# A four-layer hybrid decoder trunk on one core: small tiles moved to a pool of their own, and the activations' tiles shifted to another offset in SBUF

## The chip, the cores and the metric

The kernel runs on one core of one Trainium2 chip. The metric is the device time of one execution in microseconds. A profiled execution has a span, from its first to its last instruction, and a time of its own that is a little longer.

## The reference, cut to what matters

Four residual layers over 256 tokens of width 1024. Layer `i` has a token mixer (latent attention, a Conformer convolution module, HGRN2, attention again), then a SwiGLU feed-forward block and a gated per-layer embedding. Nearly all of the arithmetic is dense products of the 256 tokens with weights in float32:

```python
for i in range(DEPTH):
    u = _rmsnorm(h, norm1_g[i])
    h = h + mixer(u)                      # MLA, Conformer, HGRN2, MLA
    h = h + _swiglu(_rmsnorm(h, norm2_g[i]), ffn_w_gu[i], ffn_w_down[i])
    gate = jax.nn.sigmoid(_rmsnorm(h, ple_norm_g[i]) @ ple_w_gate[i])
    h = h + (p[i] @ ple_w_proj[i]) * gate
return _rmsnorm(h, final_norm_g)

def _swiglu(u, w_gu, w_down):
    gate, up = jnp.split(u @ w_gu, 2, axis=-1)
    return (jax.nn.silu(gate) * up) @ w_down
```

The widths are 1024 for the model, 2816 for the feed-forward block, 256 for the embedding.

## The kernel before, in words

The 256 tokens are two tiles of 128 rows (`NT`). The residual stream stays in SBUF as `h0` and `h1`. Every float32 product is made from three reduced-precision products: an operand is split into a high part and a low part of type `float32r`, and `mm` (L221) issues high x high, high x low and low x high into the same PSUM bank.

Weights are streamed. `granule` (L177) loads up to 1024 columns of a weight matrix into `raw` by SyncE's DMA queue; ScalarE writes the high part `whi` (L189, or L194 with the norm's gain), VectorE the low part `wlo` (L190, L195). There are 4 slots of `raw`, 9 of `whi` and 8 of `wlo`, each of 4096 bytes in a partition, in the pool `wpool`.

Activations are transposed on TensorE (`split_T`, L250) and split the same way into pairs of tiles: `xT` (the normalised stream, and the mixers' outputs), `aT` (the feed-forward block's hidden part), `cT` (attention's low-rank part) and `pT` (the embedding input). In most products a 128x128 block of an activation's tile is the stationary operand, which a weight load (LDWEIGHTS) brings into the array, and 512 columns of `whi` or `wlo` are the moving operand. In the Conformer's first product and in HGRN2's q and f projections it is the other way round: a block of the weights is stationary and 256 columns of `xT` move. Each matmul has a weight load of its own. The feed-forward block alternates, for each of 11 pieces, 24 matmuls for each token tile into the bank `mm` (from `xT`) with 12 into the banks `acc` (from `aT`).

Where the tiles lie: a pool's slots lie one behind the other in the order in which their tags are first asked for, each rounded up to 32 bytes of a partition, and the pools lie in the order in which they are opened: `const`, `wpool`, `act`, and then, at the same place again and again, the scope of the current stage. In the kernel before that gives these offsets in a partition, modulo 256 bytes:

- `whi`, `wlo`, `raw`: 224 (and all their slots, since a slot has 4096 bytes)
- `h0`, `h1`, `junk`: 224
- `xT`, `pT`, `pph`: 96
- `th`, `hg`, `gain`: 160
- the stage's scope begins at 160, and with it `aT` and `cT`

The odd offsets come from seven tags of very small tiles (one to four numbers in a partition: `ss`, `sst`, `rs_m`, `rs_y`, `rs_h`, `rs_t`, `rhalf`), which `tmp` (L158) claims from `act` among the large ones. Their 960 bytes lie partly ahead of `xT`, partly between it and `pph`, partly behind. All blocks that a matmul takes from these tiles begin at a multiple of 256 bytes from the tile's begin, so the offset of the tile is that of each block.

Of the kernel before, what the change touches and what calls it, by code (L numbers as in the profile page):

```python
# [12 lines left out]
F32 = mybir.dt.float32  # L13
# [8 lines left out]
P = 128  # L22
# [29 lines left out]
GAINS = {}  # L52
for _k in GSIZE:
    GAINS[_k] = sum(GSIZE[j] * GCOUNT[j] for j in GAINS)


class Norm:
# [3 lines left out]
    def __init__(self, T, full=False, defer=False):  # L61
        self.T, self.full, self.defer = T, full, defer
        self.x, self.r = None, [None] * NT
# [64 lines left out]
class Trunk:  # L128
    def __init__(self, ctx, tc, a, out):
        self.ctx, self.tc, self.nc, self.a, self.out = ctx, tc, tc.nc, a, out  # L130
        nc = self.nc
        pool = lambda name, **k: ctx.enter_context(tc.tile_pool(name=name, **k))
        self.const = pool("const", bufs=1)
        self.wpool = pool("wpool", bufs=1)
        self.act = pool("act", bufs=1)
        self.ps = pool("ps", bufs=1, space=PSUM)
        self.n = 0
        self.fence = []
        self.head = None
        self.pinned = False  # L140
        self.pT, self.pph = {}, {}
        self.ident = self.const.tile([P, P], F32, name="ident")
        make_identity(nc, self.ident)
        self.gT = self.const.tile([P, a["gains"].shape[1]], F32, name="gT")
        self.h = [self.act.tile([P, D], F32, name=f"h{t}", tag=f"h{t}") for t in range(NT)]

    def nm(self, s):
# [8 lines left out]
        return self.bank("acc", 4)  # L156

    def tmp(self, tag, shape, bufs, dtype=F32, pool=None):  # L158
        return (pool or self.act).tile(shape, dtype, name=self.nm(tag), tag=tag, bufs=bufs)

    def scope(self, name):
        return self.tc.tile_pool(name=name, bufs=1)
# [404 lines left out]
    def mla(self, i, norm, done, pre):  # L567
# [8 lines left out]
        with self.scope(self.nm("mla")) as pool:  # L576
# [5 lines left out]
            for t in range(NT):  # L582
                xs, r = self.cut(norm.x, t), norm.r[t]
                pa, pb = self.acc(), self.acc()
                self.mms(pa[:, :QL], xs, [(hi[:, 0, :QL], lo[:, 0, :QL]) for hi, lo in gr])
                self.mms(pb[:, : KVL + ROPE], xs, [(hi[:, 0, QL : NC + ROPE], lo[:, 0, QL : NC + ROPE]) for hi, lo in gr])
                cg = tmp("cg", [P, NC], 1)
                nc.scalar.activation(cg[:, :QL], pa[:, :QL], AF.Copy)
                V.tensor_copy(cg[:, QL:], pb[:, :KVL])
                ss = tmp("css", [P, 2], 2)  # L590
                for c, (ps, n) in enumerate([(pa, QL), (pb, KVL)]):
                    nc.scalar.activation(self.tmp("junk", [P, 512], 1, BF16)[:, :n], ps[:, :n], AF.Square, scale=r, accum_out=ss[:, c : c + 1])
                kr = tmp("kr", [P, 1, ROPE], 2)
                nc.scalar.activation(kr[:, 0], pb[:, KVL : KVL + ROPE], AF.Copy, scale=r)
                self.split_T(cg, cT, 0, t)
                css.append(ss)
                krot.append(kr)
# [579 lines left out]
```

## Time and profile before

| | |
|---|---|
| median of 3 runs | 1401.75 us (1401.49 to 1403.82) |
| the profiled execution | 1402.8 us, of which 1401.0 us are its span |
| TensorE, matmuls | 1352.4 us busy, 97% of the span, 7153 of them |
| TensorE, weight loads | 1096.6 us, 78% |
| VectorE | 919.4 us, 66% |
| ScalarE | 789.7 us, 56% |
| DMA | 228.15 MB, 163 GB/s in the mean |

A matmul's duration in the profile reaches beyond the start of the next one, since matmuls are pipelined; what a matmul costs in a stream is the distance from its start to the next one's start. The profile's timeline merges neighbours of one kind into one row with a count.

### The profile page before, as it was taken

The page shows a single profiled execution, that of the slowest core. Times are in us where ns is not written, and L with a number is a line of the kernel's source. Part 1 is how long each engine was busy: PE and PEld are TensorE (multiplying, and loading weights), DVE is VectorE, ACT ScalarE, POOL GpSimd, SP SyncE. Part 2 cuts the span into 40 slices and gives each one's busy share as a digit, 9 for nine tenths or more (in the row PEclk, how much of TensorE's full clock was granted, in tenths as well). Part 3 has the DMA queues.
Part 4 walks back from the last instruction along what each step waited for, and adds up shares of the span by engine and source line. Part 5 has one row for each costly group of instructions (what it writes and reads, how often), then busy time and mean ns, then how long its engine had stood idle before and what let it go on. Part 6 is the DMA issues. An engine that isn't in the chain of part 4 may idle for free.

```text
span 1401.0 us, 20409 instructions
## 1 busy us (share of the span) xinstructions
PE 1352.4 (97%) x7153; PEld 1096.6 (78%) x7153; DVE 919.4 (66%) x1995; ACT 789.7 (56%) x1494; POOL 19.1 (1%) x52
## 2 busy tenths in 40 slices
PE   7899999999898999999999999999999999999997
PEld 6767878887875788887788887878878767888885
DVE  6867555558876855556887768555567776655556
ACT  6776555546525654555675546555556776555543
POOL 0100000000000000000000000000000000000000
PEclk9999999999998999999999999999999999999999
DMA  7524656536564655554474425555553433665532
GB/s 234 176 67 128 201 175 191 188 123 220 182 181 153 196 181 180 181 180 163 122 211 132 133 91 175 185 181 181 180 169 110 139 121 108 217 189 187 188 119 74
DMA packets 174023, 228.15 MB, mean 163 GB/s; under 512 B 11712, under 2 KB 138848, under 8 KB 173920
## 3 DMA queue, kind: packets, MB, share of 16 engines
q1 hardware_dynamic: 173920, 226.85, 51.6%
q8 instruction: 56, 0.92, 0.3%
q14 instruction: 47, 0.39, 0.1%
HBM read 222.27 MB, written 1.05 MB: 159 GB/s over the span
## 4 chain that ended last, share of the span: by engine, by line
PE 77%; DVE 8%; DMA 6%; ACT 6%; issue 2%; SPq 0%; DVEq 0%; ACTq 0%
PE mm L216 42%; PE acc L216 26%; PE tr L259 3%; DVE wlo L195 3%; ACT whi L194 2%; DMA raw<-in_ple_w_gate_dram 1%; PE acc L1020 1%; DMA raw<-in_conv_w_pw_dram 1%; DMA raw<-in_mla_w_in_dram 1%; DMA raw<-in_ffn_w_down_dram 1%; PE acc L659 1%; ACT p L669 1%; PE tr L641 1%; DVE wlo L190 1%; ACT whi L189 1%
## 5 line engine op out<-in xcount | busy, mean ns | idle before, releaser
L216 PE MATMUL mm<-whi,xT 128*128 128x512 f32 x1632 | 553.4, 402 | 1.0 <-ACT xT L246 0.7
L194 ACT ACTIVATE whi<-raw,gT 128x512 fp32r<-128x512 f32 (+3 forms) x604 | 387.7, 700 | 136.4 <-PE acc L216 60.1
L195 DVE SCALAR_TENSOR_TENSOR wlo<-raw,gT,whi 128x512 fp32r<-128x512 f32 (+3 forms) x604 | 410.4, 729 | 60.3 <-PE acc L216 33.9
L216 PEld LDWEIGHTS mm<-whi,xT 128*128 128x128 f32 x1632 | 306.3, 189 | 67.1 <-ACT xT L246 1.2
L216 PE MATMUL mm<-wlo,xT 128*128 128x512 f32 x816 | 323.7, 397 | 1.1 <-DVE wlo L190 1.1
L216 PE MATMUL acc<-whi,aT 128*128 128x512 f32 x704 | 234.5, 394 | 1.6 <-DVE aT L247 1.6
L190 DVE TENSOR_TENSOR wlo<-raw,whi 128x1024 fp32r<-128x1024 f32 x120 | 146.4, 1223 | 73.1 <-ACT whi L189 72.7
L189 ACT ACTIVATE whi<-raw 128x1024 fp32r<-128x1024 f32 x120 | 126.1, 1059 | 97.7 <-DMA raw<-in_ffn_w_down_dram 65.9
L216 PEld LDWEIGHTS mm<-wlo,xT 128*128 128x128 f32 x816 | 154.3, 189 | 32.1 <-DVE wlo L190 1.4
L216 PE MATMUL acc<-whi,xT 128*128 128x512 f32 (+2 forms) x544 | 168.9, 386 | 2.3 <-ACT xT L246 2.1
L216 PEld LDWEIGHTS acc<-whi,aT 128*128 128x128 f32 x704 | 131.7, 188 | 34.4 <-DVE aT L247 4.0
L216 PE MATMUL acc<-wlo,aT 128*128 128x512 f32 x352 | 137.6, 391 | 0.0
L373 DVE SCALAR_TENSOR_TENSOR ga<-mm,rs_y,sg 128x256 f32<-128x256 f32 x88 | 42.3, 481 | 142.3 <-ACT sg L371 142.3
L371 ACT ACTIVATE sg<-mm,rs_y 128x256 f32<-128x256 f32 x88 | 41.0, 466 | 138.7 <-PE mm L216 138.2
L216 PEld LDWEIGHTS acc<-whi,xT 128*128 128x128 f32 x544 | 100.5, 191 | 20.4 <-ACT xT L246 2.9
L216 PE MATMUL acc<-wlo,xT 128*128 128x512 f32 (+2 forms) x272 | 103.0, 381 | 0.0
L216 PEld LDWEIGHTS acc<-wlo,aT 128*128 128x128 f32 x352 | 66.1, 188 | 14.8
L247 DVE TENSOR_TENSOR aT<-tr,aT 128x256 fp32r<-128x256 f32 x88 | 37.0, 421 | 57.7 <-ACT aT L246 57.7
L216 PEld LDWEIGHTS acc<-wlo,xT 128*128 128x128 f32 x272 | 51.7, 190 | 8.7 <-DVE wlo L195 0.2
L216 PE MATMUL mm<-whi,cT 128*128 128x384 f32 (+1 forms) x160 | 51.1, 377 | 4.9 <-ACT q L629 3.3
L82 ACT ACTIVATE junk<-h 128x512 bf16<-128x512 f32 x48 | 30.0, 625 | 40.1 <-DVE h L348 22.4
L246 ACT ACTIVATE aT<-tr 128x256 fp32r<-128x256 f32 x88 | 32.7, 371 | 29.6 <-PE tr L259 29.6
(252 smaller groups left out, 1459.8 us busy)
## 6 DMA issues: line engine op xcount, KB each, us to landing
raw<-in_ffn_w_gu_dram SPq DMA_DIRECT2D x352, 256.0 KB, 4.3
raw<-in_ffn_w_down_dram SPq DMA_DIRECT2D x88, 512.0 KB, 4.3
raw<-in_ple_w_gate_dram SPq DMA_DIRECT2D x32, 512.0 KB, 4.9
raw<-in_hgrn_w_in_dram SPq DMA_DIRECT2D x64, 256.0 KB, 3.7
raw<-in_mla_w_out_dram SPq DMA_DIRECT2D x16, 512.0 KB, 4.4
raw<-in_conv_w_pw_dram SPq DMA_DIRECT2D x32, 256.0 KB, 4.9
raw<-in_mla_w_in_dram SPq DMA_DIRECT2D x16, 336.0 KB, 4.3
raw<-in_mla_w_uq_dram SPq DMA_DIRECT2D x12, 384.0 KB, 3.7
```

The lines of the kernel that those rows point to most:

```text
L82: square = nc.scalar.activation(T.tmp("junk", [P, 512], 1, BF16), h[:, s], AF.Square, accum_out=ss[:, c : c + 1])
L189: self.last_split = nc.scalar.activation(hi[:, :used], raw[:, :used], AF.Copy)
L190: nc.vector.tensor_tensor(out=lo[:, :used], in0=raw[:, :used], in1=hi[:, :used].bitcast(F32), op=ALU.subtract)
L194: self.last_split = nc.scalar.activation(hi[:, s], raw[:, s], AF.Copy, scale=g[k])
L195: nc.vector.scalar_tensor_tensor(out=lo[:, s], in0=raw[:, s], scalar=g[k], in1=hi[:, s].bitcast(F32), op0=ALU.mult, op1=ALU.subtract)
L216: ins = self.nc.tensor.matmul(*args, **kw)
L246: a = self.nc.scalar.activation(hi, src, AF.Copy)
L247: v = self.nc.vector.tensor_tensor(out=lo, in0=src, in1=hi.bitcast(F32), op=ALU.subtract)
L259: nc.tensor.transpose(pt[:, (i - k0) * P : (i - k0 + 1) * P], src[:, i * P : (i + 1) * P], self.ident)
L371: nc.scalar.activation(sg, ps[:, :256], AF.Silu, scale=r)
L373: nc.vector.scalar_tensor_tensor(out=ga, in0=ps[:, 256:], scalar=r, in1=sg, op0=ALU.mult, op1=ALU.mult)
L641: nc.tensor.transpose(pt[:HD, h * P : (h + 1) * P], src[:, h], self.ident)
```

## The change

A new pool `small` is opened behind `act`, and `tmp` claims the seven small tags from it. Two tiles are claimed that nothing uses: `pad`, 64 bytes, the first of `small`, and `shift`, 64 bytes, the first of `act`. No instruction is added, removed or moved in the program's text.

```diff
+SMALL = ("ss", "sst", "rs_m", "rs_y", "rs_h", "rs_t", "rhalf")
+PAD = 16
...
         self.act = pool("act", bufs=1)
+        self.small = pool("small", bufs=1)
...
+        self.small.tile([P, PAD], F32, name="pad", tag="pad")
+        self.act.tile([P, 16], F32, name="shift", tag="shift")
         self.h = [self.act.tile([P, D], F32, name=f"h{t}", tag=f"h{t}") for t in range(NT)]
...
     def tmp(self, tag, shape, bufs, dtype=F32, pool=None):
-        return (pool or self.act).tile(shape, dtype, name=self.nm(tag), tag=tag, bufs=bufs)
+        return (pool or (self.small if tag in SMALL else self.act)).tile(shape, dtype, name=self.nm(tag), tag=tag, bufs=bufs)
```

## Rows read from the trace of the kernel before

**Rows 1.** The page: TensorE's line of part 1; span and granted clock of the core.
```profile
PE 1352.4 (97%) x7153; PEld 1096.6 (78%) x7153; DVE 919.4 (66%) x1995; ACT 789.7 (56%) x1494; POOL 19.1 (1%) x52
...
core 0: 1401.0 us, clock 0.992
```

**Rows 2.** The page, part 4: the chain that ended last, by engine.
```profile
PE 77%; DVE 8%; DMA 6%; ACT 6%; issue 2%; SPq 0%; DVEq 0%; ACTq 0%
```

**Rows 3.** The same chain in order of time, by line: the whole span's shares.
```profile
by line: PE mm L216 42.2%; PE acc L216 26.1%; PE tr L259 2.7%; DVE wlo L195 2.5%; issue 2.4%; ACT whi L194 1.7%; DMA raw<-in_ple_w_gate_dram 1.4%; PE acc L1020 1.1%; DMA raw<-in_conv_w_pw_dram 1.0%; DMA raw<-in_mla_w_in_dram 1.0%; DMA raw<-
```

**Rows 4.** TensorE's timeline, feed-forward block, products from `xT`: start, us, instruction, count.
```profile
477.61 0.63 PE L216 MATMUL mm<-whi,xT 128*128 128x512 f32 x2
...
479.71 0.63 PE L216 MATMUL mm<-whi,xT 128*128 128x512 f32 x2
```

**Rows 5.** The same timeline right behind, products from `aT`.
```profile
481.34 0.39 PE L216 MATMUL acc<-whi,aT 128*128 128x512 f32 x1
...
484.09 0.39 PE L216 MATMUL mm<-whi,xT 128*128 128x512 f32 x1
```

**Rows 6.** The chain's pieces in order of time: start, us, what, matmuls in it.
```profile
118.52 7.20 PE acc L216 x31
...
741.35 5.10 PE mm L216 x43
...
1375.17 16.11 PE acc L216 x69
```

**Rows 7.** Busy time by stretch: engines, granted clock (PEclk), share of the DMA engines, GB/s.
```profile
core 0: us, PE busy (x) PEld busy (x) DVE busy (x) ACT busy (x) POOL busy (x), PEclk, DMA share, GB/s
355.80:357.80 2.00, 2.00 (x10) 2.00 (x11) 2.00 (x4) 2.00 (x5) 0.47 (x1) 0.50 0.16 47
...
477.40:481.40 4.00, 4.00 (x19) 3.23 (x18) 3.54 (x7) 2.81 (x5) 0.00 (x0) 1.00 0.90 264
...
741.40:746.40 5.00, 5.00 (x45) 5.00 (x44) 4.31 (x21) 3.66 (x11) 0.00 (x0) 1.00 0.58 188
1376.00:1391.00 15.00, 15.00 (x66) 11.95 (x64) 9.72 (x33) 4.55 (x10) 0.00 (x0) 1.00 0.09 35
```

**Rows 8.** TensorE's timeline: bfloat16 matmuls of 256 columns; float32r ones just behind.
```profile
348.36 1.49 PE L216 MATMUL mm<-causal,ident_bf 128*128 128x256 bf16 x12
...
355.91 0.41 PE L216 MATMUL acc<-xT,wlo 128*128 128x256 f32 x1
...
357.83 0.41 PE L216 MATMUL acc<-xT,wlo 128*128 128x256 f32 x1
```

**Rows 9.** TensorE's groups by shape: operands, count | busy us, mean ns | idle before.
```profile
L216 PE MATMUL mm<-whi,xT 128*128 128x512 f32 x1632 | 553.4, 402 | 1.0 <-ACT xT L246 0.7 <-ACT whi L189 0.3
L216 PE MATMUL mm<-wlo,xT 128*128 128x512 f32 x816 | 323.7, 397 | 1.1 <-DVE wlo L190 1.1
L216 PE MATMUL acc<-whi,aT 128*128 128x512 f32 x704 | 234.5, 394 | 1.6 <-DVE aT L247 1.6
L216 PE MATMUL acc<-wlo,aT 128*128 128x512 f32 x352 | 137.6, 391 | 0.0
L216 PE MATMUL acc<-whi,xT 128*128 128x512 f32 x416 | 136.8, 402 | 1.0 <-ACT xT L246 1.0
L216 PE MATMUL acc<-wlo,xT 128*128 128x512 f32 x208 | 82.4, 396 | 0.0
...
L216 PE MATMUL mm<-causal,ident_bf 128*128 128x256 bf16 x12 | 1.5, 273 | 0.0
```

**Rows 10.** VectorE's groups by shape, in the same columns.
```profile
L195 DVE SCALAR_TENSOR_TENSOR wlo<-raw,gT,whi 128x512 fp32r<-128x512 f32 x512 | 356.9, 748 | 44.9 <-PE acc L216 33.3 <-ACT whi L194 10.8 <-issue 0.6
...
L348 DVE TENSOR_TENSOR h<-acc,h 128x512 f32<-128x512 f32 x26 | 17.8, 688 | 8.1 <-PE acc L216 8.1
...
L461 DVE TENSOR_TENSOR h<-h,th 128x512 f32<-128x512 f32 x16 | 11.0, 689 | 0.2
...
L124 DVE SCALAR_TENSOR_TENSOR hg<-h,rs_y,gain 128x512 f32<-128x512 f32 x4 | 2.8, 748 | 0.1
```

## The prediction

> **What bounds the kernel now.** I read the page's busy times first. TensorE's matmuls are busy for 97% of the span [rows 1], but a matmul's recorded duration overlaps the next one's, so that share alone says little. The chain that ended last says more: TensorE holds 77% of it [rows 2], and the two kinds of three-part products on L216 alone 42.2% and 26.1%, together 68.3% of 1401.0 us = 957 us [rows 3]. So the next thing to read is the distance from one matmul's start to the next one's start. The clock is no issue over the span (0.992 granted, [rows 1]).
>
> In the feed-forward block, products with `xT` as the stationary operand start at 477.61 and, 9 matmuls on, at 479.71: 2.10 us / 9 = 233.3 ns [rows 4]. The chain's long pieces agree: 7.20 us for 31 is 232.3 ns, 16.11 us for 69 is 233.5 ns [rows 6]. I use 232.8. Right behind, 12 products with `aT` take from 481.34 to 484.09: 229.2 ns [rows 5]. Both move 512 columns of the same weight tiles at the same granted clock of 1.00 [rows 7]. 512 columns at 2.4 GHz are 213.3 ns, so one pays 19.5 ns over that and the other 15.9.
>
> What is that excess? Not the other engines: in 477.40 to 481.40 the DMA engines are at 0.90, VectorE is busy 3.54 of 4.00 us, and in 1376 to 1391 DMA is at 0.09 and ScalarE at 4.55 of 15.00 us, yet the spacing is 233.3 in the one and 233.5 in the other [rows 4, 6, 7]. It also goes with how fast bytes are wanted. Twelve bfloat16 matmuls of 256 columns take 1.49 us; less the last one's 273 ns that is 1.22 / 11 = 110.9 ns, only 4.2 over the 106.7 of 256 columns [rows 8, 9]. With float32r, HGRN2's projections of 256 columns need 5.10 / 43 = 118.6 ns, 11.9 over [rows 6]. And where the granted clock is 0.50, thus 1.2 GHz, nine such float32r matmuls take 357.83 - 355.91 = 1.92 us, 213.3 ns each, exactly 256 columns and nothing over [rows 7, 8]. So only four-byte operands at 2.4 GHz pay: that looks like the two reads of TensorE (the moving columns, and the next block's weight load beside them) getting in each other's way. What differs between the `xT` and the `aT` rows is the offset between the two: `xT` begins 96 - 224, that is 128 modulo 256, from the weights, `aT` 160 - 224, that is 192. The trace of before holds no product at 64 or at 0.
>
> **The change part by part.** The change issues no instruction and no DMA, moves none past a queue, and adds no wait. What it moves is addresses. Of `act`, 960 bytes of small slots leave and 64 come in front; the rest of `act` is a multiple of 256. So everything in `act` begins at 224 + 64 = 32 modulo 256. `small` takes 64 + 960 = 1024 bytes, so the stage's scope begins at 32 too. Weights stay at 224. Every stationary activation is then 64 modulo 256 from its moving weights; where `xT` moves, the weights are 192 from it and were 128.
>
> *Stationary `xT`, 512 columns.* Counts: 1632 + 816 + 416 + 208 = 3072 [rows 9], and 96 with `pT`, by `embed`'s loops (4 layers x 2 x 2 x 2 x 3): 3168 at 128 now. Their spacing at 64 is unknown. Bounds: below, 213.3 + 4.2 = 217.5 ns, an excess as in the bfloat16 row [rows 8]; above, a third step of the size between the two rows, 232.8 + 3.6 = 236.4. I take 229.2, the `aT` row: 64 and 192 both lie one step of 64 from 128, and it is the middle of the range in which I have any row. Gain 3.6 x 3168 = 11.4 us.
>
> *Stationary `aT` and `cT`.* 704 + 352 = 1056 of `aT` [rows 9], 240 of `cT` (2 layers x 4 groups x 2 x 5 x 3), at 192 now. By the same choice they stay at 229.2: 0. Bounds: 11.7 ns less each to 7.2 ns more.
>
> *Narrower stationary products* (attention's input, 288 and 384 columns, 192 of them by the loops): the step by their mean columns, 3.6 x 336 / 512 = 2.4 ns each, 0.5 us; bounds in the same proportion.
>
> *Moving `xT`, 256 columns*: 768 by the loops (8 blocks x 2 x 8 x 3 in the Conformer and again in HGRN2). They go from 128 to 192, which for 512 columns is the better of the two known rows. Half the columns, so half the step: 1.8 ns x 768 = 1.4 us; bounds 0 and 118.6 - 110.9 = 7.7 ns each.
>
> *VectorE, ScalarE, DMA.* `h`, `th`, `hg` and `gain` move against each other too. VectorE's rows show no price for it: the addition from two SBUF tiles 64 apart takes 689 ns and the one from PSUM 688; the three-operand form takes 748 both with its SBUF inputs at the same offset (L195) and 64 apart (L124) [rows 10]. Small tiles keep their instructions. 0, with a bound of the 1 ns between those rows on some 50 instructions, nothing.
>
> Sum: 11.4 + 0 + 0.5 + 1.4 = 13.3 us of TensorE's time. How much of it reaches the end? The three-part products have about 3168 x 232.8 + 1056 x 229.2 + 240 x 200 + 192 x 160 + 768 x 120 ns = 1150 us of stream, and 957 of these are on the chain: between 0.83 and 1. Elsewhere the chain passes through weight splits and loads that would be late next. I take 0.9: 12.0 us. The profiled execution took 1402.8 us, 1.8 outside its span and 1.05 over the median; nothing here scales with that, so I take 12.0 off the median: **1389.7**.
>
> [...]
>
> **The rivals.**
>
> *64 takes nearly all of the excess away.* If the two reads then never meet, the spacing may fall towards 217.5; half-way from 229.2 is 223.4. Then 9.4 x 3168 = 29.8, 5.8 x 1056 = 6.1, `cT` 1.2, narrow 1.3, moving `xT` 3.9 x 768 = 3.0: 41.4 us, x 0.9 = 37, so 1364. All the way down it would be 15.3 x 3168 + 11.7 x 1056 + 2.4 + 2.3 + 5.9 = 71.5, x 0.9 = 64: 1337. For it: the excess is absent at 1.2 GHz and small with two-byte operands, so something does meet, and only two of the possible offsets are known. Against it: the known step from 128 to 192 is 3.6 ns of 19.5.
>
> *64 is worse than 128: slower.* If the price grows by 3.6 ns with each 64 bytes towards 0, `xT` pays 236.4 and `aT` 7.2 more: 11.4 + 7.6 + 1.4 + 0.5 = 20.9, x 0.9 = 19: 1421. If 64 is just as 128, only `aT` and `cT` lose, 3.8 + 0.7, x 0.9 = 4: 1406. The place is the feed-forward block's down products first. It decides against the change from the mean of today, (3168 x 232.8 + 1056 x 229.2) / 4224 = 231.9 ns: a spacing above that at 64 makes the kernel slower. For it: the trend of the only two rows; against it: it would have to go on past 128, and nothing says that 128 isn't the worst.
>
> *The change doesn't do what it says.* The 3.6 ns belongs to something else that separates `aT` from `xT` (where in SBUF they lie, which bank they write), or unused tiles get no room. Then 1402. Against it: `xT` into `acc` (the pieces of 31 and 69) has the spacing of `xT` into `mm` [rows 4, 6], so the bank isn't it.
>
> **How the numbers follow.** Forecast, about 1390 (1382 to 1397): 0.35. Nearly all gone, 1337 to 1382: 0.23. Same as before: 0.14. As 128, 1406: 0.12. Worse, about 1421: 0.16. A time within 0.2%, 2.8 us, is about what a measurement of this kernel can't tell from no change. Faster 0.58; same 0.15, with a little of the 1406 case; slower 0.27. The range leaves out most of the worst case and the far end of the best one: 1360 to 1412.
>
> **What the profile would show.** Right: `xT` products in the feed-forward block at about 229 ns, `aT` products still at 229, HGRN2's at 117, the same counts, VectorE's and ScalarE's means unchanged, PE's busy time down by about what the span loses. Wrong: a spacing at 64 that is none of the two known ones; `aT` slower than now; or TensorE's spacing down and the span not, with the chain's TensorE share fallen and the share of weight splits and loads risen by as much.

## The result, and the profile after

| | before | after |
|---|---|---|
| median (lowest to highest of 12 runs each) | 1401.88 us (1399.15 to 1404.43) | 1405.95 us (1402.80 to 1408.99) |
| profiled execution, and its span | 1402.8, 1401.0 | 1405.97, 1404.2 |
| TensorE's matmuls, busy | 1352.4 us | 1356.9 us |

The ratio is 1.0027, with a 95% interval from 1.0016 to 1.0038: the changed kernel is slower by 4.1 us. That is 0.27%, with an interval from 0.16% to 0.38%: about at the 0.2% at which the prediction drew its line, clear of zero, and on the other side from the forecast. The time nearly matches the small rival "64 is just as 128", for which 1406 was worked out.

The page of the kernel after, its busy times and the chain by engine, answering to [rows 1, 2]:

```profile
PE 1356.9 (97%) x7153; PEld 1094.9 (78%) x7153; DVE 919.3 (65%) x1995; ACT 788.9 (56%) x1494; POOL 17.6 (1%) x52
...
PE 81%; DVE 6%; ACT 5%; DMA 5%; issue 2%; SPq 0%; DVEq 0%; ACTq 0%
```

And its span with the granted clock:

```profile
core 0: 1404.2 us, clock 0.992
```

The counts are the same to the last instruction, the granted clock is the same, VectorE and ScalarE are busy as long as before to 0.8 us. TensorE alone is busy for 4.5 us more, and its share of the chain has risen from 77% to 81%.

TensorE's timeline of the kernel after in the feed-forward block (start, duration, instruction, count), answering to [rows 4, 5]:

```profile
477.58 0.63 PE L224 MATMUL mm<-whi,xT 128*128 128x512 f32 x2
...
479.68 0.63 PE L224 MATMUL mm<-whi,xT 128*128 128x512 f32 x2
...
480.61 0.39 PE L224 MATMUL acc<-whi,aT 128*128 128x512 f32 x1
...
483.41 0.39 PE L224 MATMUL mm<-whi,xT 128*128 128x512 f32 x1
```

Nine products from `xT` take 479.68 - 477.58 = 2.10 us, 233.3 ns each, as before. Twelve from `aT` take 483.41 - 480.61 = 2.80 us: 233.3 ns, and before it was 229.2. The chain of the kernel after, in order of time (start, us, what, matmuls), answering to [rows 6]:

```profile
120.97 7.27 PE acc L224 x31
...
743.29 4.89 PE mm L224 x43
...
1346.31 2.80 PE acc L224 x12
...
1378.35 16.12 PE acc L224 x69
```

7.27 / 31 = 234.5 and 16.12 / 69 = 233.6 ns: `xT` as stationary operand is no cheaper than before (232.3 and 233.5). 2.80 / 12 = 233.3 for `aT`. 4.89 / 43 = 113.7 ns for HGRN2's products, in which `xT` moves: cheaper (118.6 before).

The groups by shape of the kernel after (count | busy us, mean ns | idle before), TensorE's answering to [rows 9] and VectorE's to [rows 10]:

```profile
L224 PE MATMUL mm<-whi,xT 128*128 128x512 f32 x1632 | 554.6, 403 | 1.2 <-ACT xT L254 0.9 <-ACT whi L197 0.3
...
L203 DVE SCALAR_TENSOR_TENSOR wlo<-raw,gT,whi 128x512 fp32r<-128x512 f32 x512 | 356.6, 746 | 44.7 <-PE acc L224 33.7 <-ACT whi L202 10.3 <-issue 0.3
L224 PE MATMUL mm<-wlo,xT 128*128 128x512 f32 x816 | 324.5, 398 | 1.1 <-DVE wlo L198 1.1
...
L224 PE MATMUL acc<-whi,aT 128*128 128x512 f32 x704 | 236.2, 396 | 1.8 <-DVE aT L255 1.8
...
L224 PE MATMUL acc<-wlo,aT 128*128 128x512 f32 x352 | 139.2, 395 | 0.0
...
L224 PE MATMUL mm<-xT,whi 128*128 128x256 f32 x256 | 46.5, 281 | 0.0
...
L356 DVE TENSOR_TENSOR h<-acc,h 128x512 f32<-128x512 f32 x26 | 17.8, 687 | 8.8 <-PE acc L224 8.8
...
L469 DVE TENSOR_TENSOR h<-h,th 128x512 f32<-128x512 f32 x16 | 11.0, 689 | 0.2
```

The `aT` groups grew from 234.5 + 137.6 to 236.2 + 139.2 us, 3.3 together; the two large `xT` groups by 2.0; the group with `xT` moving fell from 47.6 to 46.5. VectorE's three kinds have the means of before within 2 ns. The group with `xT` moving, in the kernel before:

```profile
L216 PE MATMUL mm<-xT,whi 128*128 128x256 f32 x256 | 47.6, 284 | 0.0
```

One piece of the chain is a sample. For everything below I took all neighbours in a trace: two matmuls one behind the other, both float32r with the same number of columns, their starts less than 45 ns further apart than the columns alone take (213.3 ns for 512, 106.7 for 256). These two are an estimate from the kernel before, where matmuls start in proportion to their columns while the granted clock is 0.50: 213.3 ns apart for 256 [rows 7, 8], and 440.29 - 436.45 = 3.84 us for nine of 512, 426.7 ns each. That is 1.2 columns per ns, and the prediction's 2.4 GHz is the double of it, 2.4 columns per ns at a granted clock of 1.00. TensorE's timeline of the nine, and the stretch with its granted clock (0.50):

```profile
436.45 0.63 PE L216 MATMUL mm<-wlo,pT 128*128 128x512 f32 x1
...
440.29 0.50 PE L216 MATMUL mm<-wlo,pT 128*128 128x512 f32 x1
...
436.50:440.20 3.70, 3.70 (x10) 2.92 (x9) 2.85 (x18) 0.70 (x2) 0.00 (x0) 0.50 0.00 0
```

A pair counts for the kind of its later product. Their mean distances (about 2700 pairs for `xT`, 1040 for `aT`, 710 for the moving `xT` of 256 columns) are called *spacing* here. Before to after: `xT` 232.6 to 233.3, `aT` 229.7 to 233.3, moving `xT` 118.6 to 116.4. With the counts of the prediction: `aT` 3.6 x 1056 = 3.8 us lost, `xT` 0.7 x 3168 = 2.2 lost, moving `xT` 2.2 x 768 = 1.7 gained; `cT` and the narrow products some 0.2 lost. 4.5 us, x 0.9 = 4.1: all of the difference.

### The profile page after: what moved, and what is told of

Read it like the earlier page. It is cut to its first block, busy times and chain, and to the rows that moved or that the text cites. A ratio compares the mean times of both kernels' runs of the same rounds, so it can differ in the third digit from the quotient of the medians.

```text
span 1404.2 us, 20409 instructions
## 1 busy us (share of the span) xinstructions
PE 1356.9 (97%) x7153; PEld 1094.9 (78%) x7153; DVE 919.3 (65%) x1995; ACT 788.9 (56%) x1494; POOL 17.6 (1%) x52
## 4 chain that ended last, share of the span: by engine, by line
PE 81%; DVE 6%; ACT 5%; DMA 5%; issue 2%; SPq 0%; DVEq 0%; ACTq 0%
PE mm L224 44%; PE acc L224 27%; PE tr L267 3%; DVE wlo L203 2%; ACT whi L202 1%; DMA raw<-in_ple_w_gate_dram 1%; PE acc L1028 1%; DMA raw<-in_mla_w_in_dram 1%; PE acc L667 1%; PE tr L649 1%; DMA raw<-in_conv_w_pw_dram 1%; ACT p L677 1%; PE acc L700 1%; PE acc L1010 1%; ACT whi L197 1%
## 5 line engine op out<-in xcount | busy, mean ns | idle before, releaser
L224 PE MATMUL acc<-whi,aT 128*128 128x512 f32 x704 | 236.2, 396 | 1.8 <-DVE aT L255 1.8
L224 PE MATMUL acc<-wlo,aT 128*128 128x512 f32 x352 | 139.2, 395 | 0.0
L379 ACT ACTIVATE sg<-mm,rs_y 128x256 f32<-128x256 f32 x88 | 41.1, 467 | 139.6 <-PE mm L224 139.2
L224 PEld LDWEIGHTS acc<-wlo,aT 128*128 128x128 f32 x352 | 66.1, 188 | 15.6
```

The source lines that it names most:

```text
L224: ins = self.nc.tensor.matmul(*args, **kw)
L379: nc.scalar.activation(sg, ps[:, :256], AF.Silu, scale=r)
```

## The experiments

The theory after the result: the offset of the stationary tile from the moving one, modulo 256, sets the spacing, and 64 is a dear offset. The rivals: something else came with the change (the small tiles' new place, the addresses as such, the weights' own alignment), or the spacing isn't what the time follows. The table has all kernels that change offsets; the sections behind it take them one by one. "By spacing" is the sum of the changes of the three spacings against before, times their counts, times 0.9, without `cT` and the narrow products; "measured" is the difference of the medians to the kernel before on the same chip. Where `xT` moves, its weights lie at 256 less the offset of `xT`: with `xT` at 64 they lie 192 from it.

| kernel | `xT`, `aT` from the weights | `xT` 512, ns | `aT` 512, ns | moving `xT` 256, ns | time, us | ratio to before | by spacing, us | measured, us |
|---|---|---|---|---|---|---|---|---|
| before | 128, 192 | 232.6 | 229.7 | 118.6 | 1401.88 | | | |
| after | 64 | 233.3 | 233.3 | 116.4 | 1405.95 | 1.0027 [1.0016, 1.0038] | +3.9 | +4.1 |
| e1 | 0 | 228.3 | 227.0 | 119.8 | 1388.70 | 0.9910 [0.9890, 0.9929] | -14.0 | -13.3 |
| e2 | 128 | 232.8 | 233.1 | 118.6 | 1404.87 | 1.0020 [1.0006, 1.0033] | +3.8 | +2.8 |
| e3 | 192 | 229.2 | 229.0 | 114.7 | 1392.50 | 0.9932 [0.9912, 0.9953] | -13.1 | -9.5 |
| e4 | 192, weights on 256 | 229.2 | 229.0 | 116.4 | 1388.53 | 0.9909 [0.9886, 0.9931] | -11.9 | -13.5 |
| e5 | 32 | 233.0 | 233.4 | 117.1 | 1405.38 | 1.0021 [1.0008, 1.0034] | +3.6 | +3.7 |
| e6 | 96 | 234.0 | 234.3 | 119.9 | 1410.07 | 1.0053 [1.0030, 1.0077] | +9.3 | +8.4 |
| e7 | 160 | 233.4 | 233.4 | 117.9 | 1405.04 | 1.0031 [1.0018, 1.0045] | +5.3 | +3.3 |
| e8 | 224 | 233.1 | 233.4 | 118.3 | 1403.80 | 1.0017 [1.0002, 1.0032] | +4.7 | +2.1 |
| e9 | 64, 192 | 233.4 | 230.5 | 117.4 | 1404.04 | 1.0021 [1.0006, 1.0035] | +2.2 | +2.5 |
| e11 | 192, 0 | 229.2 | 228.5 | 114.8 | 1391.94 | 0.9944 [0.9921, 0.9966] | -13.5 | -9.6 |
| e12 | 192, 0, weights on 256 | 229.1 | 228.6 | 114.8 | 1388.33 | 0.9906 [0.9885, 0.9928] | -13.7 | -13.2 |
| e14 | 0, weights on 256 | 228.3 | 227.0 | 119.8 | 1387.62 | 0.9904 [0.9888, 0.9919] | -14.0 | -14.0 |

In every row the sign by spacing is the sign measured, and the two differ by at most 3.9 us. So the rival that the time doesn't follow the spacing falls; those on the addresses are taken below. The factor of 0.9 is rough: in the seven kernels whose spacings add up to more than 10 us, the time took between 0.64 (e11) and 1.02 (e4) of them.

One more rival: ScalarE, VectorE and the DMA engines write the weights' slots at the same distances from `xT`, and it might be their accesses that TensorE meets. The traces speak against it. Where no instruction of VectorE, ScalarE or GpSimd runs from 300 ns before the first start of a pair to 200 ns after the second (about 400 pairs of `xT` in each trace), the spacing is 233.5 ns in the changed kernel, 227.1 in e1 and 228.7 in e3. With no DMA packet beside them either, it is 233.7 (63 pairs) in the changed kernel and 226.8 (37) in e1. So the difference is there with no other engine at work beside TensorE.

### e1: the small pool, without the shift (offset 0)

```diff
-        self.act.tile([P, 16], F32, name="shift", tag="shift")
```

> The changed kernel without the 64 bytes of the tile shift: every activation's tile then begins at the weights' offset, 0 modulo 256 apart. Theory R (the distance of the stationary block from the moving weights, modulo 256, sets the spacing of the 512-column products; 233.4 ns at 64, 232.8 at 128, 229.2 at 192 in the two traces): a spacing of its own, the same for xT and aT; if the price goes on growing towards 0, about 237 ns and 1418 us; if 0 lies beside 192 on the circle, 229 to 232 and 1390 to 1402. Theory S (the small tiles' own pool cost the time, the offset nothing): as the changed kernel, 1406 us, xT 233, aT 233.

Measured: 1388.70 us (1387.99 to 1390.22), 13.3 under before. The page's busy line of e1:

```profile
PE 1336.7 (96%) x7153; PEld 1092.8 (79%) x7153; DVE 918.6 (66%) x1995; ACT 788.8 (57%) x1494; POOL 17.7 (1%) x52
```

And its chain (start, us, what, matmuls):

```profile
732.84 5.16 PE mm L223 x43
...
1328.93 2.72 PE acc L223 x12
...
1360.77 15.72 PE acc L223 x69
```

16.12 us for 69 products become 15.72: 227.8 ns. 2.80 for twelve of `aT` become 2.72: 226.7. Only the moving `xT` lost, 120.0 ns in the piece of 43 (113.7 after). TensorE is busy for 20.2 us less than in the changed kernel, VectorE and ScalarE as long. One tile of 64 bytes that nothing reads is the whole difference between a fast placement and a slow one; the small tiles' new place is thus no cause of the loss.

### e2 and e3: the shift made 128 and 192 bytes

```diff
-        self.act.tile([P, 16], F32, name="shift", tag="shift")
+        self.act.tile([P, 32], F32, name="shift", tag="shift")
```

This is e2; e3 has 48 in place of 32.

> The changed kernel with 128 bytes in the tile shift: every activation's tile begins 128 from the weights. Theory R: xT and aT both at 232.4 to 232.8 ns, as xT was before; aT's 1056 products lose 3.5 ns each against before, the moving xT go back to 118.6, so about 1404 us. Theory S: 1406 us whatever the offset, spacings as in the changed kernel.

> The changed kernel with 192 bytes in the tile shift: every activation's tile begins 192 from the weights, as only aT and cT did before. Theory R: xT and aT both at 229.2 ns; 3168 products x 3.6 ns, 192 narrower ones x 2.4, times 0.9, so about 11 us under before: 1391 us. The moving xT are then 64 from the weights' block, unknown, within 2 us. Theory S: 1406 us. Theory T (what separates aT from xT is the tile, its place or its bank): xT stays at 232 to 233 and the time at 1402.

Measured: 1404.87 us and 1392.50 us. The chain of e2:

```profile
1345.04 2.80 PE acc L224 x12
...
1377.27 16.06 PE acc L224 x69
```

And the chain of e3:

```profile
735.71 4.90 PE mm L224 x43
...
1333.28 2.75 PE acc L224 x12
...
1365.52 15.83 PE acc L224 x69
```

With everything at 128 both kinds of product have before's `xT` spacing (16.06 / 69 = 232.8, 2.80 / 12 = 233.3), and with everything at 192 both have before's `aT` spacing (229.4 and 229.2). So the two rows of the trace of before were read rightly: it is the offset, and not that one product comes from `xT` and the other from `aT`. What e2 loses is nearly `aT` alone, 3.4 x 1056 = 3.6 us. In e3 the moving `xT` gained more than the 2 us that were allowed for it, 3.9 x 768 = 3.0, and yet the time fell by less than the spacings give (9.5 of 13.1 us); why isn't shown.

### e5 to e8: the odd multiples of 32

The same line with 8, 24, 40 and 56 in place of 16.

> The changed kernel with 32 bytes in shift: activations 32 from the weights, so that the blocks begin at a multiple of 64 and the weights don't. Theory R with steps of 64 (pieces of 64 bytes are what meets): as 0 or as 64, 227 or 233 ns for 512 columns, 1389 or 1406 us. Theory R with a smooth dependence: between them, about 230 ns and 1397 us.

> The changed kernel with 96 bytes in shift. Steps of 64: as 64 or 128, 232.6 to 233.3 ns, 1404 to 1406 us. Smooth: 233 ns, the top of the curve, 1405 us.

> The changed kernel with 160 bytes in shift. Steps of 64: as 128 or 192, 232.6 or 229.1 ns, 1404 or 1391 us. Smooth: 231 ns, 1398 us.

> The changed kernel with 224 bytes in shift. Steps of 64: as 192 or 0, 229.1 or 227 ns, 1391 or 1389 us. Smooth: 228 ns, 1390 us.

Measured: 1405.38, 1410.07, 1405.04 and 1403.80 us, all slower than before. The chain of e6, the slowest:

```profile
1351.23 2.82 PE acc L224 x12
...
1383.57 16.18 PE acc L224 x69
```

16.18 / 69 = 234.5 ns. The chain of e8, at 224:

```profile
1226.92 2.80 PE acc L224 x12
...
1379.56 16.12 PE acc L224 x69
```

16.12 / 69 = 233.6 and 2.80 / 12 = 233.3 ns. The four spacings of `xT` are 233.0 to 234.0, of `aT` 233.4 to 234.3. So of eight offsets two are cheap, 0 and 192, and the six others lie within 1.7 ns of each other (`xT` and `aT` together 232.6 to 234.3). Neither a curve that rises smoothly from 0 nor steps of 64 bytes with the same price inside a step gives this: 224 lies between the two cheap ones and is dear.

### e9: `aT` and `cT` put back to 192, `xT` left at 64

```diff
-PAD = 16
+PAD = 48
```

> The changed kernel with 192 instead of 64 bytes in pad: xT and pT stay 64 from the weights, aT and cT go back to the 192 they had before. Theory R: xT 233.3 ns, aT 229.1 ns; the changed kernel less 4.2 ns x 1056 and the same on cT, 5 us: 1401 us, no different from before. If the loss of the change lay elsewhere than in aT and cT: 1406 us.

Measured: 1404.04 us, 2.5 over before. The chain of e9:

```profile
1342.76 2.76 PE acc L224 x12
...
1374.98 16.14 PE acc L224 x69
```

`aT` is back at 2.76 / 12 = 230.0 ns while `xT` stays at 16.14 / 69 = 233.9: the two are set one by one. 2.8 ns less for `aT` than in the changed kernel, x 1056 x 0.9, is 2.7 us; moving `xT`, 1.0 ns more, takes 0.7 of it: 2.0 were due, and the time stands 1.6 us nearer to the kernel before (2.5 over it in place of 4.1). The intervals of the two ratios overlap, so the spacing shows this part and the time alone doesn't. The expected return to the time of before didn't come: the interval of the ratio begins at 1.0006, since `xT` stays 0.8 ns dearer than before and `aT` is still at 230.5, not 229.1.

### e11: the shift alone, without the small pool

To the kernel before, one line is added:

```diff
+        self.act.tile([P, 16], F32, name="shift", tag="shift")
         self.h = [self.act.tile([P, D], F32, name=f"h{t}", tag=f"h{t}") for t in range(NT)]
```

> The other part of the change alone: the 64 bytes of shift, and the small tiles left among the large ones as before. h lies 64 from the weights, xT and pT 192, aT and cT 0. Theory R: xT 229.1 and aT 227.0 ns as in the runs at 192 and at 0, the moving xT at 114.7 as in the run at 192: 3168 x 3.4 + 1056 x 2.7 + 768 x 3.9 = 16.6 us, x 0.9 = 15 under before: 1387 us. Theory S (the pool of its own carries the gain of the run at 0): no gain, 1402 us.

Measured: 1391.94 us, 9.6 under before. The chain of e11:

```profile
1329.97 2.73 PE acc L222 x12
...
1362.07 15.83 PE acc L222 x69
```

This moves `xT` from 128 to 192 (229.4 ns) and `aT` from 192 to 0 (227.5). The expectation of a gain without the pool came; of the 15 us expected 9.6 did, 3.9 less than the spacings of the table give, and why isn't shown. Each half of the change alone makes the kernel faster, e1 by 13.3 us and e11 by 9.6, since each takes both tiles to a cheap offset; the two together add up to 64 and lose.

### e4, e12, e14: the weights on a multiple of 256 bytes

One line is added to e3, e11 and e1; 32 bytes ahead of everything take the weights from 224 to 0:

```diff
+        self.const.tile([P, 8], F32, name="cshift", tag="cshift")
         self.ident = self.const.tile([P, P], F32, name="ident")
```

> As the kernel with 192 bytes in shift, and 32 unused bytes ahead of the constants, so that the weights' tiles begin at a multiple of 256 and the activations' at 192 modulo 256. Theory R: only the distance counts, 229.2 ns for both, 1391 us as without it. Theory A (where a tile itself lies modulo 64 counts too: so far all operands begin 32 behind a multiple of 64): 512 columns are then 32 pieces of 64 bytes and not parts of 33, so up to 6.7 ns less, 222.5 ns and 1391 - 27 = 1364 us.

> As the shift alone, with 32 unused bytes ahead of the constants, so that weights begin at a multiple of 256, and all distances stay. Theory R: the same, 1387 us. If the 4 us between the two runs at 192 came from where the weights lie, 1383 us.

> As the run at offset 0, with 32 unused bytes ahead of the constants, so that the weights and all activations begin at multiples of 256. Theory R (the distance alone): 227 to 228 ns and 1388.7 us, as without it. If weights on a multiple of 256 are worth the 4 us of the other two pairs: 1384.7 us, with the same spacing.

Measured: 1388.53, 1388.33 and 1387.62 us, against 1392.50, 1391.94 and 1388.70 without the 32 bytes: 4.0, 3.6 and 1.1 us. All addresses move by 32, no offset between two of them changes. The chain of e14:

```profile
1327.94 2.72 PE acc L224 x12
...
1359.73 15.70 PE acc L224 x69
```

15.70 / 69 = 227.5 and 2.72 / 12 = 226.7, as in e1: it is the offset that counts and not the address, to within 0.1 ns for `xT` and `aT` in all three pairs. The 222.5 ns of e4's second theory didn't come. The ranges of e3 and e4 lie apart (1390.11 to 1393.29 and 1387.98 to 1389.97); those of e11 and e12 overlap (1389.41 to 1395.21 and 1384.55 to 1390.07), and so do those of e1 and e14 (1387.99 to 1390.22 and 1385.62 to 1390.49). So only the first pair's 4.0 us are clear of the noise, and where they come from isn't settled. In the profiled executions the stretches at a granted clock of 0.50 add up, within the span, to 26.1 us in e3 and 19.2 in e4. In the kernel before a product of 512 columns took 426.7 ns at 0.50 and 232.6 in the mean of the pairs, so the 6.9 us more of it may cost 6.9 x (1 - 232.6 / 426.7) = 3.1 us, an estimate; but these are one execution of each. e14 has the lowest median of all, 14.0 us under the kernel before; that it is below e1, e4 or e12 is not shown.

### e10 and e13: which of the two reads pays

In e1's placement, one of the three products was put 64 off. e10 gives the low part of `xT` tiles of its own, 64 bytes further:

```diff
-        return tuple(self.tmp(tag, [P, nk, S], bufs, F32R, pool) for _ in range(2))
...
+        hi = self.tmp("xT", [P, nk, S], 2, F32R)
+        if not self.gap:
+            self.gap = self.act.tile([P, 16], F32, name="gap1", tag="gap1")
+        lo = self.tmp("xTl", [P, nk, S], 2, F32R)
...
+        return hi, lo
```

e13 moves `wlo` by 192 bytes, so that `xT` and `aT` lie 64 from `wlo` and 0 from `whi` (64 bytes behind `raw` bring `act` back to its place):

```diff
         hi = self.tmp("whi", [P, 1024], 9, F32R, pool=self.wpool)
+        if not self.gap:
+            self.wpool.tile([P, 48], F32, name="gap1", tag="gap1")
         lo = self.tmp("wlo", [P, 1024], 8, F32R, pool=self.wpool)
...
```

> The kernel with offset 0, but the low parts of xT in slots of their own 64 bytes further, so that in each triple of matmuls the third one's stationary block is 64 from the weights and the other two are at 0. Theory L (what meets the moving columns is the load of the next matmul's block): the matmul before the third, which moves wlo, is slow, about 233 ns to the next start, and the other two are at 227. Theory O (the block's own matmul pays): the third, which moves whi with the low block, is slow, 233, and the one that moves wlo stays at 227. Either way about 2 ns more per xT product in the mean, 6 us, 1394 us.

> The kernel with offset 0, but the slots of wlo 192 bytes further (modulo 256), so that the stationary blocks lie 0 from whi and 64 from wlo: in each triple the middle matmul, which moves wlo, is at 64 with its own block and with the next one's. If the record of starts doesn't lag: the distance from its start to the next start is the slow one, about 233 to 236, the other two 227 to 229. If it lags by one: the slow one is that of the third matmul, whi with the low block, as in the run with the low parts 64 away, and then both theories of who pays are open again. Sum as there: about 2 ns per product in the mean, and 1396 us, since aT pays too.

Measured, one run each: 1397.15 us (1394 expected) and 1395.16 us (1396 expected). TensorE's timeline of e10 in the last products:

```profile
1374.81 0.40 PE L224 MATMUL acc<-whi,xTl 128*128 128x512 f32 x1
1375.05 0.39 PE L224 MATMUL acc<-whi,xT 128*128 128x512 f32 x1
1375.28 0.39 PE L224 MATMUL acc<-wlo,xT 128*128 128x512 f32 x1
1375.51 0.40 PE L224 MATMUL acc<-whi,xTl 128*128 128x512 f32 x1
```

The long interval, 0.24, is the one behind the start of the product whose own block lies 64 away (`xTl`). Over the whole trace: 233.6 ns behind it, 229.3 and 229.2 behind the two others. The interval in which the block 64 away is loaded for the next product, that of `wlo`, is not the long one (a load runs in the interval ahead of its product: in the changed kernel that of a `wlo` product begins at 477.82 and takes 0.19 us, and the product begins at 478.05). By that it would be the running product's own pair of operands that pays. e13 then should show a long interval behind each `wlo` product, whose own block and whose next one are both 64 away. TensorE's timeline of e13 in the same place:

```profile
1374.08 0.39 PE L228 MATMUL acc<-wlo,xT 128*128 128x512 f32 x1
...
1376.83 0.39 PE L228 MATMUL acc<-wlo,xT 128*128 128x512 f32 x1
```

Four triples in 2.75 us, 229.2 ns for each product, and over the whole trace 230.3 behind `wlo` and 229.4 behind `whi`. So no single interval is dear in e13, and neither "the load of the next block pays" nor "the own pair pays" fits both kernels. Nor can a single interval decide it. In e11, where `xT` lies at 192 and `aT` at 0, the step from a `whi` product of `xT` to one of `aT` takes 234.9 ns (84 pairs) and the step back 225.8 (75), beside 228 to 230 within either kind; in e1, with both at 0, the same two steps take 227.1 and 226.7. So an interval depends here on the offsets of both products that bound it, and a long one doesn't tell whose operands pay. Whether one read waits for another, and which, no run shows.

## Why the prediction was wrong

Step by step, in its own order.

- **What bounds the kernel: right.** Of the engines' busy times only TensorE's moved by more than 2 us, and the time went the way of the spacing in every row of the table, to within 3.9 us.
- **That the offset modulo 256 sets the spacing: right.** e2 and e3 bring both products to either of the two rows of before; e14 keeps the offsets, moves the addresses and keeps the spacing. It holds for `xT` and `aT`; `cT`, which the prediction put with `aT`, isn't cheap at 0 (last section).
- **The price at 64: the step that failed.** "I take 229.2, the `aT` row: 64 and 192 both lie one step of 64 from 128." It measured 233.3. The term of 11.4 us for stationary `xT` became a loss of 2.2, and the zero for `aT` and `cT` a loss of 3.8 and a little. The choice rested on a circle on which 64 and 192, one step to either side of 128, cost the same. The measured prices don't have that symmetry: 192 and 64 differ by 4.1 ns, and 224, one step of 32 below 0 and from 192, is as dear as 128. No row of before bore on it. A third offset was taken to equal the better of two known ones, with nothing that kept it from the dearer one; e1 to e8 show that six of eight offsets are dear.
- **The bounds: held.** 233.3 lies between 217.5 and 236.4, and 1405.95 inside the range; the break-even of 231.9 decided as it said. The rival "64 is just as 128", 1406 by "only `aT` and `cT` lose", is what came: `aT` lost the 3.8 us that it gave. That the time met it to 0.1 us is partly luck: `xT` lost 2.2 us and the moving `xT` gained 1.7, both of which that rival left out. Its chance of 0.12 was too small beside 0.35 for the forecast. (The bfloat16 row of the lower bound is 110.2 ns by its eleven starts, 3.5 over the columns; the prediction had 110.9 and 4.2 from rounded times.)
- **64 takes nearly all away: fell.** 0 is the cheapest offset seen, 227.0 for `aT`, still 13.7 ns over the 213.3 of the columns.
- **Moving `xT`: right in sign and mis-sized.** 1.4 us were expected, 2.2 x 768 = 1.7 came. But that the order of the prices carries over from the 512-column products isn't so: moving `xT` is dearest at 0 and 160 from its weights (119.8 and 119.9) and cheapest at 64 (114.7).
- **No price on VectorE, ScalarE and DMA: right**, by the means above; TensorE's two largest waits are what they were (6.4 us for `hg`, before 6.3, and 4.7 for the load of `h`).
- **The pass-through of 0.9: held here, and only roughly elsewhere.** 4.5 us of spacing gave 4.1; e1's 15.6 us gave 13.3, 0.85, but e3's 14.5 gave 9.5, 0.66, and e4's 13.2 gave 13.5.
- **The change does nothing: fell.** The same 7153 matmuls and loads at the same granted clock (0.992 and 0.993) are busy for 1356.9 us with the stationary tiles 64 from the weights and 1336.7 with them at 0. That two reads of TensorE get in each other's way was the prediction's conjecture from [rows 6, 7, 8]; no run shows it, nor that it is the load which takes from the matmul (e10 and e13).

## What to carry to other kernels

Where back-to-back float32r matmuls bound a kernel, compare their start-to-start distance between streams that differ in nothing but their tiles' addresses: a few ns there times thousands of matmuls is a gain that costs no instruction, and a small tile claimed between two large ones can give or take it (here 64 bytes took `xT` from 228.3 to 233.3 ns and `aT` from 227.0 to 233.3, and the time from 13.3 us under before to 4.1 over it). Measure the offsets, all of them, rather than reason from two known ones by symmetry; here both halves of a change were gains (13.3 and 9.6 us) and their sum was a loss. Put such tiles (one number in a partition, odd sizes) in a pool of their own first, so that the large tiles keep the offset that they were given.

## What the runs showed of the hardware

All of it is measured on this kernel and its variants: mean spacings of one trace each, at a granted clock of 0.990 to 0.993 over the span.

- Stationary activations against 512 moving columns of float32r, by the offset of the two tiles modulo 256 bytes: 0 gives 227.0 to 228.6 ns (e1, e11, e12, e14), 192 gives 229.0 to 229.2 (e3, e4, e11, e12; 229.7 before and 230.5 in e9 for `aT`, where `xT` lies elsewhere and is dear), and 32, 64, 96, 128, 160 and 224 give 232.6 to 234.3 (before, after, e2, e5 to e9). These numbers are those of `xT` and `aT`. That 224, between the two cheap ones, is dear was the least expected of it.
- `cT`, a stationary tile of the same kind in shorter streams, doesn't share the gain at 0: its products of 384 columns (90 to 93 pairs in a trace) take 174.9 to 175.6 ns at 0 (e1, e11, e12, e14), 175.0 at 64 and 175.5 at 128, and 173.3 to 173.5 at 192 (before, e3, e4, e9); those of 512 columns (53 or 54 pairs) 231.2 to 232.6 at 0 and 230.7 to 231.5 at 192. Why, isn't known.
- With `xT` moving (256 columns) and the weights stationary the order is another one: the weights 64 from `xT` cost 114.7 to 114.8 ns in three kernels (e3, e11, e12) and 116.4 in a fourth (e4), 192 costs 116.4 (after) and 117.4 (e9), 128 costs 118.6 (before, e2), 0 costs 119.8 (e1, e14), 160 costs 119.9 (e6). e4 has the offset of e3 and not its spacing; why, isn't known.
- Not settled: whether one of TensorE's reads waits, and which (e10 against e13), what the 4.0 us between e3 and e4 are, and why the time of e3 and e11 fell by less than their spacings give.
